# Moving the 1/rms multiply of gate and up to GpSimd in half of the feed-forward tiles

## The chip, the cores and the metric

The kernel runs on one core of a Trainium2 chip. The metric is the time of one execution on the device in microseconds (us). A core has engines that run side by side, each through its own instructions in order: TensorE (PE; its weight loads are shown as PEld), VectorE (DVE), ScalarE (ACT), GpSimd (POOL) and SyncE (SP), which here issues the loads. They wait for each other by semaphores. SBUF is the on-chip memory; PSUM is the small memory that TensorE writes its sums to.

## The reference

Two layers over 256 tokens of width 1024, in float32. Layer 0 mixes tokens with a short gated convolution, layer 1 with causal attention of 16 heads; each is followed by the same feed-forward, with 2816 gate and 2816 up channels:

```python
def conv_ffn(h, w_up, w_conv, w_down):
    gu = causal_dwconv(h @ w_up, w_conv)
    g, u = jnp.split(gu, 2, axis=-1)
    return (jax.nn.silu(g) * u) @ w_down

x = x + conv_ffn(rmsnorm(x, ffn_norm[i]), ffn_w_up[i], ffn_w_conv[i], ffn_w_down[i])
```

`rmsnorm` multiplies each token by 1/rms and each channel by a gain. The factor 1/rms belongs to the token, so it can be applied after the matmul with `w_up`, to gate and up, as long as it comes before the convolution over tokens.

## The kernel before

Activations lie with channels on the 128 partitions and the 256 tokens along the row. Each float32 matmul operand is split into a high and a low part, `hi` and `lo`, and three products are summed (high by high, high by low, low by high). Weights come from memory in units of 128 x 1024. `split_next` makes the two parts of the next unit: ScalarE copies it to `hi`, VectorE subtracts (`lo<-raw,hi`, the weight subtraction; both inputs in SBUF). Five units may be in flight (`SPLITS`), so VectorE can work ahead of TensorE by a few units and no more.

`ffn` (lines 660 to 727) runs both feed-forwards in 22 tiles `j` of 128 gate and 128 up channels. For a tile TensorE does the gate matmuls, the up matmuls, and from tile 4 on (`LAG_FFN`) the down projection of tile `j - 4`. Behind each of these pieces stands a `slot()`: it emits one `split_next`, and then the next step of every open task, oldest first. The steps of a tile are two generators:

- `gathered(j, h)`, once for gate and once for up: ScalarE copies one half of the PSUM sum into `gn`, VectorE adds the other half (`gn<-gu,gn`, one input in PSUM). After the add TensorE may use that PSUM bank again; there are banks for two tiles.
- `whole(j)`: first step, the multiply of `gn` by 1/rms (`gn<-gn,rstd`, 128 x 512, gate and up in one instruction). Second step, `taps`: ScalarE writes the first tap of gate and of up to `gy`, VectorE adds the two other taps (four `gy<-gn,sm,gy`, both tensor inputs in SBUF). Third: silu on ScalarE (`s`), times up on VectorE (`p`). Fourth: `p` is split for the down projection (`ps_jh` on ScalarE, `ps_jl` on VectorE).

So the multiply of tile `j` is emitted right behind the add of its up half; the next slot brings a weight subtraction and then the taps. The multiplies of tiles 0 and 1 are emitted together, since 1/rms (`rstd`) is ready only in tile 1. `V`, `S`, `G`, `E`, `Q` are VectorE, ScalarE, GpSimd, TensorE and SyncE, each wrapped in `InOrder`, which keeps the order of emission on that engine. GpSimd has one other job, eight multiplies by 1/rms in the mixer of layer 0 (`mix_cv`, line 591: `y<-y,rstd`, 128 x 256).

The multiply and what follows it (lines 676 to 679):

```python
            V.tensor_mul(gn, gn, nm.r[:, None, :].to_broadcast([P, 2, T]))
            yield
            taps(*((y[:, h, :], gn[:, h, :], partial(ffn_tap, layer, half=h, j=j)) for h in range(2)))
            yield
```

Of the kernel before, what the change touches and what calls it, by code (L numbers as in the profile page):

```python
# [15 lines left out]
P = 128  # L16
D = 1024
T = 256
# [4 lines left out]
NF = DFF // P  # L23
# [114 lines left out]
def trunk(ctx: ExitStack, tc: tile.TileContext, x, wall, small, ropes, masks, final, out):  # L138
    nc = tc.nc
    V, S, G, E, Q = (  # L140
        InOrder(tc, e) for e in (nc.vector, nc.scalar, nc.gpsimd, nc.tensor, nc.sync)
    )
# [103 lines left out]
    def unit(key):  # L246
        u = INDEX[key]
        while state["split"] <= u:
            split_next()
        return hi[u], lo[u]  # L250
# [4 lines left out]
    def spawn(*gens):  # L255
        tasks.extend(gens)

    def slot(splits=1, ahead=True):

        for _ in range(splits if ahead else 0):  # L260
            split_next()
        for g in sorted(tasks, key=lambda g: (g.__name__ == "rotate") == ahead):
            if next(g, StopIteration) is StopIteration:
                tasks.remove(g)
        for _ in range(0 if ahead else splits):
            split_next()

    def bank(name, tag="b"):
        return pp.tile([P, 2, T], F32, name=name, tag=tag, bufs=4)
# [68 lines left out]
    def table(func):  # L338

        t = line(ap_, 1, name="table", tag="table", bufs=1)  # L340
        S.activation(t, ones[:, 0:1], func)

    def finish_norm(i, nm, squared=False, tag="b"):

        ps = bank(f"ss{i}", tag=tag)
        for part, total in enumerate(nm.total):
            E.matmul(
                ps[:, 0, :], ones_r, total, start=part == 0, stop=part == 1, skip_group_check=True
            )
        rms = line(ap_, T, name=f"rms{i}", tag="rms", bufs=1)  # L350
        S.activation(rms, ps[:, 0, :], AF.Sqrt, bias=eps, scale=1.0 / D)
        nm.r = line(ap_, T, name=f"rstd{i}", tag="rstd", bufs=2)
        V.reciprocal(nm.r, rms)
        if squared:
            nm.r2 = ap_.tile([P, T], F32, name=f"rstd2{i}", tag="rstd2", bufs=1)
            V.tensor_mul(nm.r2, nm.r, nm.r)
# [29 lines left out]
    def project_both(dst, w, nm, ks=range(ND)):  # L386

        wh, wl = w
        kw = {"skip_group_check": True}
        for k in ks:  # L390
            s = slice(k * P, (k + 1) * P)
            E.matmul(
                dst.rearrange("p c t -> p (c t)"), wh[:, s], nm.both[k], start=k == 0, stop=False, **kw
            )
            E.matmul(dst[:, 0, :], wl[:, s], nm.xh[k], start=False, stop=k == ND - 1, **kw)
# [121 lines left out]
    def split_act(h, l, v):  # L517
        S.activation(h, v, AF.Copy)
        V.tensor_sub(l, v, h.bitcast(F32))

    def half_tile(name):
        return ap_.tile([P, T], F32, name=name, tag="t", bufs=NT)

    def pair_tile(name):
        return ap_.tile([P, 2, T], F32, name=name, tag="big", bufs=NBIG)

    def split_turned(name, v):

        h, l = (turned(name=name + c, tag="ps" + c, bufs=NPS) for c in "hl")
        split_act(h.places, l.places, by_place(v))  # L530
        return h.columns, l.columns

    def split_tiles(name, kind):
        return tuple(
            line(ap_, T, INPUTS_AT[kind], F32R, name=name + c, tag="ps" + c, bufs=NPS) for c in "hl"
        )

    def taps(*parts):

        for y, src, w in parts:  # L540
            S.activation(y, src, AF.Copy, scale=w(2))
        for t in (1, 0):
            o = 2 - t
            for y, src, w in parts:
                V.scalar_tensor_tensor(
                    y[:, o:], src[:, : T - o], w(t), y[:, o:], op0=ALU.mult, op1=ALU.add
                )
# [105 lines left out]
    nm = Norm()  # L653
# [6 lines left out]
    def ffn(layer, nm, i, then):  # L660
        acc, ps = (TokenAccum if then is None else Accum)(f"fo{layer}"), {}
        gus = {}
        tag = "ab"[then is not None]

        gns = {}

        def gathered(j, h):

            S.activation(gns[j][:, h, :], gus[j][h][:, 1, :], AF.Copy)
            V.tensor_add(gns[j][:, h, :], gus[j][h][:, 0, :], gns[j][:, h, :])  # L670
            yield

        def whole(j):
            gn, y = gns.pop(j), pair_tile(f"gy{layer}_{j}")
            s, p = half_tile(f"s{layer}_{j}"), half_tile(f"p{layer}_{j}")
            V.tensor_mul(gn, gn, nm.r[:, None, :].to_broadcast([P, 2, T]))
            yield
            taps(*((y[:, h, :], gn[:, h, :], partial(ffn_tap, layer, half=h, j=j)) for h in range(2)))
            yield
            S.activation(s, y[:, 0, :], AF.Silu)  # L680
            V.tensor_mul(p, s, y[:, 1, :])
            yield
            if layer == 0:
                ps[j] = split_turned(f"ps{layer}_{j}", p)
                return
            ps[j] = split_tiles(f"ps{layer}_{j}", f"down{layer}")
            split_act(*ps[j], p)

        for j in range(NF):
            if layer == 0 and j == 2:  # L690
                Q.dma_start(rope, ropes)
                Q.dma_start(mk, masks)
            gu = gus[j] = [bank(f"gu{layer}_{j}_{h}", tag=tag) for h in range(2)]
            gns[j] = pair_tile(f"gn{layer}_{j}")
            wg, wu = unit(("up", layer, 0, j)), unit(("up", layer, 1, j))
            if j == 0:
                for ks in ((0, 1), (2, 3), (4, 5), (6, 7)):
                    project_both(gu[0], wg, nm, ks)
                    project_both(gu[1], wu, nm, ks)
                spawn(gathered(0, 0), gathered(0, 1))  # L700
                if then is None:
                    spawn(turn(acc))
                slot()
                slot()
            else:
                project_both(gu[0], wg, nm)
                spawn(gathered(j, 0))
                slot()
                project_both(gu[1], wu, nm)
                spawn(gathered(j, 1))  # L710
                if j == 1:
                    finish_norm(i, nm, tag=tag)
                    table(AF.Silu)
                    spawn(whole(0))
                spawn(whole(j))
                slot()
            if j >= LAG_FFN:
                acc.add(("down", layer, j - LAG_FFN), ps[j - LAG_FFN], j == LAG_FFN, False)
                slot()
        last = range(NF - 2 - (then is None), NF)  # L720
        for j in range(NF - LAG_FFN, last[0]):
            acc.add(("down", layer, j), ps[j], False, False)
            slot()
        while tasks:
            slot(0)
        table(AF.Sqrt)
        acc.finish([("down", layer, j) for j in last], [ps[j] for j in last], then)
# [8 lines left out]
    nm = nm2  # L736
# [226 lines left out]
    def turn(acc):  # L963
        turn_pair(3)
        yield
        rows = blocks.rearrange("p (t q) m a -> p t q (m a)", t=2)
        moved = rest["moved"]
        for i in range(4):
            for q in range(4):
                Q.dma_start(  # L970
                    moved[32 * q : 32 * q + 32, :, i * T : (i + 1) * T], rows[32 * i : 32 * i + 32, :, q]
                )
            if i % 2:
                yield
        for _ in range(3):
            yield
        for t in range(2):
            for h in range(2):
                acc.seed(t, h, moved[:, t, h * 2 * T : (h + 1) * 2 * T])
            yield  # L980

    nm = Norm()
# [111 lines left out]
```

## Time and profile before

| | |
|---|---|
| median of 3 runs | 552.97 us (552.54 to 553.43) |
| profiled execution | 553.03 us |
| its span, first to last instruction | 551.1 us |
| TensorE busy in the span | 542.3 us (98%) |
| VectorE busy | 493.9 us (90%) |
| ScalarE busy | 370.9 us (67%) |
| GpSimd busy | 8.7 us (2%) |
| feed-forward of layer 0 / layer 1 | about 92 to 268 us / 372 to 545 us |

In a table of stretches the last three columns are the granted TensorE clock, the DMA share and GB/s. Rows of a timeline give the start in us from the span's start, the duration in us, the engine, the line, the operation, the tile that it writes and those that it reads, shapes, and a count where neighbours of one kind are merged; a bracket tells idle time of the engine in front of it and what ended it. Recorded neighbours on one engine overlap by about 0.08 us. All instructions carry line 121, that of the wrapper, so they are told apart by tiles. In the name `gn<-gn,rstd`, `rstd` is 1/rms.

### The profile page before, as it was taken

To read this page: it belongs to the slowest core of one execution; us is meant where nothing else is said; L and a number is where in the kernel's file an instruction comes from. 1 tells how busy PE (TensorE), PEld (TensorE's weight loads), DVE (VectorE), ACT (ScalarE), POOL (GpSimd) and SP (SyncE) were. 2 spreads that over 40 slices of the span, in tenths; PEclk is the share of its full clock that TensorE was granted. 3 is DMA by queue.
4 is the path that set the end of the run, shared out by engine and by line. 5 is a ranking of instruction groups with operands and counts; after the bars stand their busy time and mean duration, and the time that the engine had idled before them with its cause. 6 is when DMAs were issued, how large, how long until landed. Compare 5 with 4: busy or idle time off the path is not lost.

```text
span 551.1 us, 10100 instructions
## 1 busy us (share of the span) xinstructions
PE 542.3 (98%) x3911; PEld 509.0 (92%) x3911; DVE 493.9 (90%) x879; ACT 370.9 (67%) x652; POOL 8.7 (2%) x12
## 2 busy tenths in 40 slices
PE   8999999999999999999999999999999999999995
PEld 8999999889999999999999998999899999999985
DVE  6999777999999999999899887589999999889984
ACT  6746446767777766767856666677777777666655
POOL 0022000000000000000000000000000000000000
PEclk9999999999999999999999999999999999999998
DMA  8947653545665556556266244455665666655402
GB/s 294 399 165 292 228 173 144 205 161 213 227 217 216 219 200 223 195 188 227 84 225 230 78 153 153 154 211 218 208 219 212 218 221 222 223 195 188 152 0 79
DMA packets 18753, 107.85 MB, mean 196 GB/s; under 512 B 2192, under 2 KB 4880, under 8 KB 6544
## 3 DMA queue, kind: packets, MB, share of 16 engines
q1 hardware_dynamic: 18272, 106.65, 53.8%
q8 instruction: 31, 0.51, 0.3%
q10 hardware_dynamic: 432, 0.54, 0.3%
q14 instruction: 18, 0.15, 0.1%
HBM read 105.09 MB, written 1.05 MB: 193 GB/s over the span
## 4 chain that ended last, share of the span: by engine, by line
PE 87%; DVE 9%; ACT 1%; issue 1%; DMA 1%; SPq 0%; DVEq 0%; ACTq 0%
PE gu L121 33%; PE fo L121 20%; PE qk L121 8%; PE cv L121 7%; DVE lo L121 4%; PE ao L121 4%; PE v L121 4%; PE b L121 4%; PE mo L121 3%; DVE gy L121 2%; PE s L121 1%; DVE gn L121 1%; PE o L121 1%; PE pt L121 1%; DMA raw<-wall 1%
## 5 line engine op out<-in xcount | busy, mean ns | idle before, releaser
L121 DVE TENSOR_TENSOR lo<-raw,hi 128x1024 fp32r<-128x1024 f32 (+3 forms) x201 | 239.0, 1195 | 23.3 <-ACT hi L121 22.6
L121 ACT ACTIVATE hi<-raw 128x1024 fp32r<-128x1024 f32 (+2 forms) x199 | 205.2, 1040 | 51.6 <-PE gu L121 15.6
L121 PE MATMUL gu<-x,hi 128*128 128x512 f32 x704 | 233.0, 382 | 0.9 <-DVE gn L121 0.9
L121 PE MATMUL gu<-x,lo 128*128 128x256 f32 x704 | 192.1, 273 | 0.1
L121 PEld LDWEIGHTS gu<-x,hi 128*128 128x128 f32 x704 | 133.1, 189 | 19.3 <-DVE gn L121 1.5
L121 PEld LDWEIGHTS gu<-x,lo 128*128 128x128 f32 x704 | 135.1, 192 | 1.2 <-DVE lo L121 0.7
L121 DVE SCALAR_TENSOR_TENSOR gy<-gn,sm,gy 128x254 f32<-128x254 f32 (+1 forms) x176 | 72.9, 476 | 0.6 <-ACT gy L121 0.6
L121 ACT ACTIVATE gy<-gn,sm 128x256 f32<-128x256 f32 x88 | 39.8, 501 | 30.2 <-DVE gn L121 30.2
L121 PE MATMUL cv<-x,hi 128*128 128x256 f32 x256 | 44.5, 277 | 0.5 <-ACT hi L121 0.5
L121 PE MATMUL qk<-x,hi 128*128 128x256 f32 x256 | 43.8, 277 | 0.1
L121 ACT ACTIVATE gn<-gu 128x256 f32<-128x256 f32 x88 | 32.4, 371 | 14.9 <-PE gu L121 14.9
L121 PEld LDWEIGHTS cv<-x,hi 128*128 128x128 f32 x256 | 39.2, 193 | 0.8 <-ACT hi L121 0.7
L121 PEld LDWEIGHTS qk<-x,hi 128*128 128x128 f32 x256 | 38.8, 192 | 0.7 <-issue 0.6
L121 DVE TENSOR_TENSOR gn<-gu,gn 128x256 f32<-128x256 f32 x88 | 36.6, 418 | 0.6
L121 PE MATMUL qk<-x,lo 128*128 128x256 f32 x128 | 35.2, 275 | 0.0
L121 PE MATMUL cv<-x,lo 128*128 128x256 f32 x128 | 32.7, 277 | 0.4 <-DVE lo L121 0.4
L121 DVE TENSOR_TENSOR gn<-gn,rstd 128x512 f32<-128x512 f32 x44 | 30.2, 691 | 1.4
L121 ACT ACTIVATE s<-gy 128x256 f32<-128x256 f32 x44 | 18.2, 414 | 18.5 <-DVE gy L121 18.4
L121 PE MATMUL b<-x,hi 128*128 128x256 f32 x128 | 25.1, 275 | 0.0
L121 PEld LDWEIGHTS qk<-x,lo 128*128 128x128 f32 x128 | 24.6, 192 | 0.0
L121 PEld LDWEIGHTS cv<-x,lo 128*128 128x128 f32 x128 | 23.5, 193 | 0.6 <-DVE lo L121 0.6
L121 ACT ACTIVATE sm<-sm,nmx 128x256 f32<-128x256 f32 (+1 forms) x32 | 14.1, 442 | 12.5 <-DVE nmx L121 12.5
(484 smaller groups left out, 958.4 us busy)
## 6 DMA issues: line engine op xcount, KB each, us to landing
raw<-wall SPq DMA_DIRECT2D x95, 1024.0 KB, 4.8
raw<-wall SPq DMA_DIRECT2D x6, 384.0 KB, 6.5
late<-vts SPq DMA_DIRECT2D x16, 64.0 KB, 2.0
raw<-wall SPq DMA_DIRECT2D x3, 192.0 KB, 3.9
xt<-x SPq DMA_DIRECT2D x2, 256.0 KB, 6.2
late<-final SPq DMA_DIRECT2D x1, 512.0 KB, 5.6
out<-of SPq DMA_DIRECT2D x2, 256.0 KB, 2.2
rope<-ropes SPq DMA_DIRECT2D x1, 384.0 KB, 6.4
```

Of the source, the lines that this page charges most:

```text
L121: r = f(*args, **kw)
```

## The change

In tiles 0 to 10 of both feed-forwards (`NF` is 22) the multiply by 1/rms goes to GpSimd; in tiles 11 to 21 VectorE does it as before. Nothing else is touched: the same instruction on the same tiles, emitted at the same place.

```diff
-            V.tensor_mul(gn, gn, nm.r[:, None, :].to_broadcast([P, 2, T]))
+            (G if j < NF // 2 else V).tensor_mul(gn, gn, nm.r[:, None, :].to_broadcast([P, 2, T]))
```

## Rows read from the trace of the kernel before

**Rows 1.** The page, part 1: busy us (share of span), instructions, by engine.

```profile
PE 542.3 (98%) x3911; PEld 509.0 (92%) x3911; DVE 493.9 (90%) x879; ACT 370.9 (67%) x652; POOL 8.7 (2%) x12
```

**Rows 2.** Stretches: from:to, length, busy us (instructions) of PE, PEld, DVE, ACT, POOL.

```profile
97.00:110.00 13.00, 12.93 (x80) 11.66 (x79) 12.90 (x18) 9.40 (x16) 0.00 (x0) 1.00 0.60 214
110.00:133.00 23.00, 22.58 (x152) 20.77 (x151) 22.90 (x45) 16.14 (x32) 0.00 (x0) 1.00 0.49 180
...
150.00:175.00 25.00, 25.00 (x178) 23.65 (x177) 24.86 (x44) 18.00 (x32) 0.00 (x0) 1.00 0.65 239
...
380.00:394.00 14.00, 13.36 (x83) 12.06 (x82) 14.00 (x23) 9.50 (x18) 0.00 (x0) 1.00 0.49 149
...
480.00:532.00 52.00, 52.00 (x297) 47.14 (x296) 47.60 (x81) 35.04 (x60) 0.00 (x0) 1.00 0.42 154
```

**Rows 3.** Groups by line: instruction, count | busy us, mean ns | idle before.

```profile
L121 DVE TENSOR_TENSOR gn<-gn,rstd 128x512 f32<-128x512 f32 x44 | 30.2, 691 | 1.4
```

**Rows 4.** Timeline of POOL in the mixer; columns: start us, us, instruction.

```profile
33.04 0.73 POOL L121 TENSOR_TENSOR y<-y,rstd 128x256 f32<-128x256 f32 x1 [0.42 <-DVE y L121]
36.24 1.58 POOL L121 TENSOR_TENSOR y<-y,rstd 128x256 f32<-128x256 f32 x1 [2.47 <-DVE y L121]
```

**Rows 5.** Timeline of DVE beside those two multiplies.

```profile
33.26 0.42 DVE L121 TENSOR_TENSOR cv<-cv,cn 128x256 f32<-128x256 f32 x1
33.60 1.25 DVE L121 TENSOR_TENSOR lo<-raw,hi 128x1024 fp32r<-128x1024 f32 x1
...
36.01 1.22 DVE L121 TENSOR_TENSOR lo<-raw,hi 128x1024 fp32r<-128x1024 f32 x1
37.14 0.95 DVE L121 TENSOR_TENSOR ys0l<-yb,ys0h 128x256 fp32r<-128x256 f32 x1
```

**Rows 6.** Timeline of DVE around the multiply of tile 8, layer 0.

```profile
156.78 0.43 DVE L121 TENSOR_TENSOR gn<-gu,gn 128x256 f32<-128x256 f32 x1
157.25 0.69 DVE L121 TENSOR_TENSOR gn<-gn,rstd 128x512 f32<-128x512 f32 x1
157.85 1.22 DVE L121 TENSOR_TENSOR lo<-raw,hi 128x1024 fp32r<-128x1024 f32 x1
158.99 1.66 DVE L121 SCALAR_TENSOR_TENSOR gy<-gn,sm,gy 128x255 f32<-128x255 f32 x4
160.57 1.22 DVE L121 TENSOR_TENSOR lo<-raw,hi 128x1024 fp32r<-128x1024 f32 x1
```

**Rows 7.** Timeline of ACT behind that multiply: the first taps.

```profile
157.97 0.91 ACT L121 ACTIVATE gy<-gn,sm 128x256 f32<-128x256 f32 x2 [1.18 <-DVE gn L121]
```

**Rows 8.** Timeline of DVE around the multiply of tile 3, layer 0.

```profile
122.06 0.41 DVE L121 TENSOR_TENSOR gn<-gu,gn 128x256 f32<-128x256 f32 x1
...
126.22 0.45 DVE L121 TENSOR_TENSOR gn<-gu,gn 128x256 f32<-128x256 f32 x1
```

**Rows 9.** Timeline of DVE around the multiplies of tiles 0 and 1, layer 0.

```profile
106.69 1.16 DVE L121 TENSOR_TENSOR lo<-raw,hi 128x1024 fp32r<-128x1024 f32 x1
...
108.10 1.28 DVE L121 TENSOR_TENSOR gn<-gn,rstd 128x512 f32<-128x512 f32 x2
...
113.59 0.41 DVE L121 TENSOR_TENSOR gn<-gu,gn 128x256 f32<-128x256 f32 x1
```

**Rows 10.** Timeline of PE: the first matmul with each of three lo units.

```profile
133.48 0.38 PE L121 MATMUL gu<-x,lo 128*128 128x256 f32 x1
...
181.10 0.27 PE L121 MATMUL gu<-x,lo 128*128 128x256 f32 x1
...
462.28 0.38 PE L121 MATMUL fo<-lo,ps_8h 128*128 128x512 f32 x1
```

**Rows 11.** Timeline of DVE: the subtractions that wrote those three units.

```profile
132.20 1.22 DVE L121 TENSOR_TENSOR lo<-raw,hi 128x1024 fp32r<-128x1024 f32 x1
...
174.74 1.22 DVE L121 TENSOR_TENSOR lo<-raw,hi 128x1024 fp32r<-128x1024 f32 x1
...
454.06 1.22 DVE L121 TENSOR_TENSOR lo<-raw,hi 128x1024 fp32r<-128x1024 f32 x1
```

## The prediction

> **What bounds the kernel now.** The page comes first: TensorE is busy for 98% of the span and VectorE for 90% [rows 1]. With both so full, a share says nothing; what matters is who waits for whom, stage by stage. The table by stretches shows that TensorE loses time in two places of the feed-forwards only, at the start of each [rows 2]: 12.93 of 13.00 us busy from 97 to 110, 22.58 of 23.00 from 110 to 133, 13.36 of 14.00 from 380 to 394. VectorE has no gap there (14.00 of 14.00). From 150 to 175 TensorE is full and VectorE still has no gap; from 480 to 532 VectorE has 4.4 us to spare. So VectorE enters each feed-forward late, is just fast enough, works its way ahead of TensorE, and idles once its buffers are full. The first eleven tiles, where the change acts, are the ones in which it has no gap.
>
> How fast it gains is read from one tile in its order of time [rows 6]. The weight subtraction behind tile 8's taps starts at 160.57 us, the one behind tile 10's at 174.74 [rows 11]: 7.1 us a tile. TensorE first uses the one behind tile 4's taps at 133.48 and that behind tile 10's at 181.10 [rows 10]: 7.9 us a tile. VectorE gains 0.8 us a tile. Behind tile 4 its slack is nothing (132.20 + 1.22 = 133.42, used at 133.48); behind tile 10 it is 181.10 - 175.96 = 5.14 us. In layer 1 the subtraction behind tile 10's taps ends at 455.28 and is first used at 462.28: 7.00 us. (Which subtraction feeds which matmul is found by counting, since both engines take the weight units in the plan's order.)
>
> **What is removed.** 11 multiplies in each layer, 0.69 us each [rows 3]. They take 0.64 us from the add's end to the start of the next instruction (157.21 to 157.85) [rows 6], 22 x 0.64 = 14.1 us of VectorE.
>
> **What is added, and what GpSimd's rows say of it.** GpSimd does the same kind of multiply in the mixer, at half this size [rows 4]. Undisturbed it takes 0.73 us (at 33.04). Issued while VectorE runs a weight subtraction it takes 1.58 (at 36.24, one of three such), and ends 0.59 after that subtraction (37.82 against 37.23) [rows 4, 5]. So it waits for that instruction, and then needs 0.59. The reverse shows as well. Behind the subtraction at 36.01, the next VectorE instruction, ys0l, is issued at 37.14 and takes 0.95, where cv, of the same size, takes 0.42; it ends 0.28 after GpSimd is done. The subtraction at 33.60 ends 1.08 after the GpSimd multiply that ran when it was issued. But a VectorE instruction with one operand in PSUM, cv at 33.26, is not lengthened beside that multiply. Two SBUF operands on VectorE and a GpSimd multiply exclude each other for a whole instruction, and a GpSimd multiply that waits gets in between two VectorE instructions.
>
> The Trainium skill has two wordings of this. "Advanced Engine Details and Errata", section VectorE Performance Modes, names GpSimd interference for VectorE's two-port modes alone; by it these float32 two-input instructions would run undisturbed, and the change would give the faster rival below. "SBUF — State Buffer", section Who interferes with whom, adds VectorE instructions with two SBUF inputs against a GpSimd instruction that reads SBUF. The 0.95 us of ys0l decides for the second.
>
> **The multiply's length at 512 elements** is in no row. Call C the time it holds VectorE off once a running subtraction ends. Upper bound: 1.46, twice the undisturbed 0.73. Proportional to the 0.59: 1.18. Lower bound: 0.59 plus what 256 more elements cost VectorE, 0.69 - 0.41 = 0.28, so 0.87. I take 1.15, just under proportional: the 0.14 by which 0.73 exceeds 0.59 is a fixed part already taken out, and it equals VectorE's own fixed part (2 x 0.41 - 0.69 = 0.13). By "GPSIMD Engine Reference" of the Trainium skill, section Elementwise — side-by-side cycle accounting (2048 elements in 4497 ns, an estimate of 2.2 ns each), C would also be 1.15 and the sum the same; no run here shows it.
>
> **One tile worked through (tiles 5 to 10).** Let T be the end of the add that completes gn (157.21 in rows 6). Now: multiply, subtraction, four taps, next subtraction at 160.57 = T + 3.36. After the change VectorE, which issues in order, goes straight to the subtraction, at T - 0.08 (neighbours overlap by 0.08). GpSimd starts some 0.23 behind it (36.24 against 36.01 in the mixer), finds the subtraction running, and gets in at T + 1.14. It ends at T + 1.14 + C. ScalarE's first tap starts 0.03 later, as it does now behind the multiply [rows 7], and takes 0.50; VectorE's taps start 0.03 after that and need 1.58 to the next subtraction (158.99 to 160.57). That lands at T + 3.28 + C. VectorE loses C - 0.08 = 1.07 us a tile, 6.4 in six tiles. What waits behind the taps on VectorE is the next weight subtraction, and TensorE waits for that one. ScalarE's next weight copy, queued behind its two taps, ends near T + 3.0 + C, before VectorE asks for it; that costs nothing as long as it stays under T + 3.28 + C.
>
> **Tiles 3 and 4** have a ps subtraction of some 0.4 us between weight subtraction and taps, which fills part of the wait. Now the next instruction comes at 126.22, with T = 122.47: T + 3.75 [rows 8]. After: T + 3.28 + C again. Loss C - 0.47 = 0.68 each, 1.4 for the two. Tile 2 has two ps subtractions; with another 0.38 hidden it loses 0.3.
>
> **Tiles 0 and 1** are multiplied back to back at 108.10 [rows 9], and the add that lets TensorE go on comes at 113.59. After: GpSimd takes tile 0 when the subtraction ends at 107.85, until 109.00. The next subtraction, held off, ends 1.08 later, at 110.08. GpSimd takes tile 1 until 111.23. The first tap ends 0.28 after it, seven more follow at 0.395, and the add starts at 114.20: 0.6 late. Dropping two multiplies (1.3) has not paid for two exclusions (2.3), less what a PSUM add and the overlaps hide.
>
> **The sum.** VectorE is behind its present schedule by 0.6 + 0.3 + 1.4 + 6.4 = 8.7 us after tile 10. Layer 0: 8.7 less the slack of 5.14 is 3.55 us of TensorE waiting, most of it early, where the slack is nothing. Layer 1, by the same tile costs: 8.7 - 7.00 = 1.7. From tile 11 on VectorE has its multiply back and catches up 0.8 a tile for eleven tiles, which just covers it; I cost the end of the layer at nothing, and if the cover fails it is tenths of a us. Together 5.2. The profiled execution took 553.03 (span 551.1 and 1.9 around it), level with the median of 552.97: **558.2 us**.
>
> **Bounds.** Each 0.1 us of C is 2.2 us of the result while both layers are late. C = 0.87 gives 8.7 - 3.1 = 5.6 us behind: 0.5 to 0.8 us in layer 0, nothing in layer 1, 553.7. C = 1.46 gives 12.1 behind: 7.0 + 5.1, so 565.
>
> **Rivals.**
> 1. Faster: no exclusion at this operand shape, GpSimd runs beside VectorE. Its multiply would end near T + 0.15 + 1.3 = T + 1.45, the taps start near T + 2.0 against T + 1.78 now (157.21 to 158.99): 0.2 lost a tile in tiles 5 to 10, which the slack hides, and 1.3 us won at tiles 0 and 1, where TensorE waits. The gain is at most what TensorE loses there, 0.07 + 0.42 + 0.64 = 1.1 us [rows 2]: 551.9. It decides if a VectorE instruction with two SBUF operands keeps its length beside a GpSimd multiply. For it: VectorE is the late engine in just these tiles. Against: ys0l's 0.95. Chance 0.09.
> 2. No change: C is near its lower bound, so slack swallows nearly all: 553.5. For it: nothing but the lack of a 512-element row. Chance 0.08.
> 3. Forecast, slower: 0.83. In it, about 0.08 lies above 563: C near 1.4, or VectorE's ps subtraction getting in ahead of GpSimd, or the end of a layer not caught up.
>
> The range that holds 8 in 10 leaves out the faster rival and the top: 554.5 to 563. A measurement of this kernel can tell about 0.2%, 1.1 us, from no change; the chances for faster, the same and slower by that are 0.09, 0.08 and 0.83.
>
> **What would show it.** On the page: 22 GpSimd multiplies gn<-gn,rstd of about 2.1 us each (0.15 after T to T + 2.29), where 1.3 would mean no exclusion. VectorE idle in front of the first tap, ended by ScalarE's tap, some 1.7 us a tile in tiles 5 to 10. Weight subtractions and taps themselves little longer than now, since the loss is waiting. TensorE waiting for lo in tiles 4 to 11 of layer 0 and less in layer 1. From tile 11 on, tiles of the present length. Wrong would be: subtractions beside GpSimd at 1.22 us with GpSimd at 1.3 (rival 1), or a layer 1 that loses as much as layer 0 (its slack misread).

## The result, and the profile after

The changed kernel takes 560.82 us (560.61 to 561.30) against 552.78 us in the same comparison: ratio 1.0145, 95% interval 1.0133 to 1.0157, 8.0 us slower. The forecast was 558.2, 5.2 us slower, in a range of 554.5 to 563. The profiled execution took 560.87 us, its span is 558.6.

Three lines of the page after: busy time by engine (as [rows 1]), then two groups, with busy us, mean ns of one, and the idle time in front of them.

```profile
PE 545.6 (98%) x3911; PEld 508.9 (91%) x3911; DVE 483.6 (87%) x857; ACT 368.1 (66%) x652; POOL 57.2 (10%) x34
...
L121 DVE SCALAR_TENSOR_TENSOR gy<-gn,sm,gy 128x254 f32<-128x254 f32 (+1 forms) x176 | 75.1, 489 | 28.2 <-ACT gy L121 28.2
...
L121 POOL TENSOR_TENSOR gn<-gn,rstd 128x512 f32<-128x512 f32 x22 | 48.5, 2208 | 334.9 <-DVE rstd L121 233.1
```

VectorE fell from 90 to 87% busy, and TensorE stayed at 98%: the shares would let one expect a gain. The second line has the cost. In front of the taps VectorE now sits idle for 28.2 us, ended by ScalarE's first tap. GpSimd's multiply of 128 x 512 is recorded with 2.2 us. The taps in the kernel before, with 0.6 us of idle time:

```profile
L121 DVE SCALAR_TENSOR_TENSOR gy<-gn,sm,gy 128x254 f32<-128x254 f32 (+1 forms) x176 | 72.9, 476 | 0.6 <-ACT gy L121 0.6
```

The table by stretches (columns as in [rows 2]; layer 1 begins 4.5 us later than before):

```profile
97.00:110.00 13.00, 12.90 (x80) 11.65 (x79) 12.90 (x17) 9.05 (x15) 3.21 (x2) 1.00 0.62 216
110.00:133.00 23.00, 20.87 (x139) 18.74 (x138) 20.18 (x37) 13.28 (x26) 8.48 (x4) 1.00 0.45 158
133.00:150.00 17.00, 15.99 (x111) 14.61 (x111) 12.84 (x22) 10.94 (x20) 4.63 (x3) 1.00 0.53 198
150.00:175.00 25.00, 25.00 (x174) 23.06 (x173) 19.75 (x35) 16.30 (x30) 6.44 (x3) 1.00 0.56 189
390.00:404.00 14.00, 12.82 (x79) 11.58 (x78) 12.83 (x20) 8.09 (x18) 7.03 (x3) 1.00 0.58 189
480.00:532.00 52.00, 52.00 (x297) 47.23 (x296) 51.76 (x90) 38.08 (x68) 0.00 (x0) 1.00 0.57 209
```

TensorE was busy 20.87 of 23.00 us from 110 to 133 (before 22.58), 15.99 of 17.00 from 133 to 150 (before 16.93), and 12.82 of 14.00 from 390 to 404 (before, from 386 to 400, 13.36). VectorE had no gap in these tiles before; from 150 to 175 it now works 19.75 of 25.00 us, and yet it is what TensorE waits for. At the end of layer 1 (480 to 532) it has no idle time left (51.76 of 52.00, before 47.60): it is catching up.

One tile of the changed kernel, tile 7 of layer 0, beside [rows 6] (a tile of the same kind): GpSimd's timeline, with tile 3's multiply above it, and then VectorE's.

```profile
123.74 2.52 POOL L121 TENSOR_TENSOR gn<-gn,rstd 128x512 f32<-128x512 f32 x1 [4.46 <-DVE gn L121]
...
155.54 2.12 POOL L121 TENSOR_TENSOR gn<-gn,rstd 128x512 f32<-128x512 f32 x1 [6.01 <-DVE gn L121]
```

```profile
154.98 0.41 DVE L121 TENSOR_TENSOR gn<-gu,gn 128x256 f32<-128x256 f32 x1
155.31 1.21 DVE L121 TENSOR_TENSOR lo<-raw,hi 128x1024 fp32r<-128x1024 f32 x1
158.24 1.67 DVE L121 SCALAR_TENSOR_TENSOR gy<-gn,sm,gy 128x255 f32<-128x255 f32 x4 [1.72 <-ACT gy L121]
159.82 1.22 DVE L121 TENSOR_TENSOR lo<-raw,hi 128x1024 fp32r<-128x1024 f32 x1
```

The add ends at 155.39 = T. VectorE starts the weight subtraction at once, GpSimd at 155.54; the subtraction ends at 156.52, GpSimd's multiply at 157.66, 1.14 us after it. The taps start at 158.24, after 1.72 us without work, and the next subtraction at 159.82 = T + 4.43. Before, it came at T + 3.36.

Where TensorE waits: first its wait for the add behind tiles 0 and 1 of layer 0 in the kernel before, then all its waits over 0.5 us in the feed-forwards of the changed kernel, and one of the short ones late in layer 1 (timeline of TensorE; the bracket is idle time and what ended it; the last row has none because the modelled end of the matmul before it hides the gap of 0.19):

```profile
114.06 0.48 PE L121 MATMUL gu<-x,hi 128*128 128x512 f32 x1 [0.27 <-DVE gn L121]
```

```profile
114.57 0.48 PE L121 MATMUL gu<-x,hi 128*128 128x512 f32 x1 [0.85 <-DVE gn L121]
...
130.03 0.38 PE L121 MATMUL fo<-ps_1h,lo 128*128 128x256 f32 x1 [1.07 <-DVE lo L121]
...
136.69 0.38 PE L121 MATMUL gu<-x,lo 128*128 128x256 f32 x1 [1.01 <-DVE lo L121]
...
398.94 0.48 PE L121 MATMUL gu<-x,hi 128*128 128x512 f32 x1 [1.18 <-DVE gn L121]
...
406.67 0.48 PE L121 MATMUL fo<-hi,ps_0h 128*128 128x512 f32 x1 [0.93 <-ACT fo L121]
...
469.67 0.48 PE L121 MATMUL fo<-lo,ps_8h 128*128 128x512 f32 x1
```

The length of a feed-forward's gate and up work, from the start of its first such matmul to that of its last, shows by layer where time went. The stretch from there to the next stage was 13.5 and 13.3 us (within 0.1), and the middle between the feed-forwards 103.7, in every kernel here but one. The first two rows differ by 4.6 and 2.95 us, which leaves 0.3 of the 7.8 between the two profiled executions. Outside the spans they differ by 0.4 (2.26 against 1.89 us; other kernels here had 1.78 to 2.11), and no run explains that. The medians are from three comparisons, in which the kernel before took 552.78 to 552.90 us; each difference below is taken within one of them. How far VectorE is behind is read from the same weight subtraction in two kernels, each time counted from the start of the layer's gate and up work.

| kernel (GpSimd multiplies in tiles ...) | median us | layer 0, us | layer 1, us |
|---|---|---|---|
| before (none) | 552.9 | 162.59 | 160.34 |
| after (0 to 10) | 560.82 | 167.18 | 163.29 |
| t0_1 (0, 1) | 554.03 | 163.12 | 160.89 |
| t2_4 (2 to 4) | 557.33 | 165.30 | 161.54 |
| t5_10 (5 to 10) | 554.26 | 163.87 | 160.35 |
| t11_16 (11 to 16) | 552.88 | 162.58 | 160.35 |
| t11_20 (11 to 20) | 562.91 | 162.57, then 6.0 late | 160.35, then 4.5 late |
| dead_mul | 559.48 | 166.73 | 162.64 |
| dead_set | 552.78 | 162.63 | 160.32 |
| later_g (2 to 10) | 553.60 | 163.00 | 160.35 |
| later_v (none) | 552.04 | 161.84 | 160.35 |
| later_v1 (none) | 551.38 | 161.77 | 159.52 |

### The profile page after: what moved, and what is told of

Same layout as the page of the kernel before. It is cut to its first block, busy times and chain, and to the rows that moved or that the text cites. A ratio compares the mean times of both kernels' runs of the same rounds, so it can differ in the third digit from the quotient of the medians.

```text
span 558.6 us, 10112 instructions
## 1 busy us (share of the span) xinstructions
PE 545.6 (98%) x3911; PEld 508.9 (91%) x3911; DVE 483.6 (87%) x857; ACT 368.1 (66%) x652; POOL 57.2 (10%) x34
## 3 DMA queue, kind: packets, MB, share of 16 engines
HBM read 105.09 MB, written 1.05 MB: 190 GB/s over the span
## 4 chain that ended last, share of the span: by engine, by line
PE 85%; DVE 7%; ACT 3%; POOL 2%; issue 1%; DMA 1%; SPq 0%; DVEq 0%; ACTq 0%; POOLq 0%
PE gu L121 32%; PE fo L121 20%; PE qk L121 8%; PE cv L121 7%; PE ao L121 4%; PE v L121 4%; PE b L121 4%; PE mo L121 3%; DVE lo L121 3%; POOL gn L121 2%; DVE gy L121 2%; ACT hi L121 1%; PE s L121 1%; PE o L121 1%; DMA raw<-wall 1%
## 5 line engine op out<-in xcount | busy, mean ns | idle before, releaser
L121 DVE SCALAR_TENSOR_TENSOR gy<-gn,sm,gy 128x254 f32<-128x254 f32 (+1 forms) x176 | 75.1, 489 | 28.2 <-ACT gy L121 28.2
L121 POOL TENSOR_TENSOR gn<-gn,rstd 128x512 f32<-128x512 f32 x22 | 48.5, 2208 | 334.9 <-DVE rstd L121 233.1
L121 ACT ACTIVATE s<-gy 128x256 f32<-128x256 f32 x44 | 18.3, 416 | 13.3 <-DVE gy L121 12.5
```

The source lines that it names most:

```text
L121: r = f(*args, **kw)
```

## The experiments

**Is it the exclusion, or the wait for GpSimd's result?** Two kernels leave VectorE's multiplies where they were and add a GpSimd instruction behind the taps, where nothing reads `gn` any more. In the first it repeats the multiply, in the second it writes zeros.

```diff
             taps(*((y[:, h, :], gn[:, h, :], partial(ffn_tap, layer, half=h, j=j)) for h in range(2)))
+            if j < NF // 2:
+                G.tensor_mul(gn, gn, nm.r[:, None, :].to_broadcast([P, 2, T]))
             yield
```

> VectorE keeps all multiplies. In tiles 0 to 10 GpSimd repeats the multiply on gn behind the taps, where nobody reads gn any more, so that nothing waits for GpSimd's result and the output is the same. A (exclusion): each holds back one VectorE instruction with two SBUF operands by some 1.1 us (less what a PSUM add hides, 0.3), without giving 0.64 back, so VectorE loses 0.8 to 1.1 a tile: 9 to 12 us late, less 5.15 and 7.0 of slack: +4 to +12, centre +7, 560. Theory C (what costs is the wait for GpSimd's result through ScalarE, not the exclusion): nothing waits, 0, 552.8.

Measured: 559.48 us, ratio 1.0121 (1.0106 to 1.0135), 6.6 slower, near the centre of theory A. Nothing waits for this multiply, and yet it costs nearly as much as the change: exclusion costs time by itself. GpSimd and VectorE in tile 5 of layer 0:

```profile
137.46 2.47 POOL L121 TENSOR_TENSOR gn<-gn,rstd 128x512 f32<-128x512 f32 x1 [5.71 <-ACT s L121]
```

```profile
137.23 1.22 DVE L121 TENSOR_TENSOR lo<-raw,hi 128x1024 fp32r<-128x1024 f32 x1
138.37 0.42 DVE L121 TENSOR_TENSOR p<-s,gy 128x256 f32<-128x256 f32 x1
138.70 0.42 DVE L121 TENSOR_TENSOR gn<-gu,gn 128x256 f32<-128x256 f32 x1
139.03 1.98 DVE L121 TENSOR_TENSOR lo<-raw,hi 128x1024 fp32r<-128x1024 f32 x1
```

The subtraction at 137.23 and p behind it keep their lengths, and GpSimd waits. It gets in at about 138.79, where p (both inputs in SBUF) ends and the add, with one input in PSUM, runs its usual 0.42. The next subtraction takes 1.98 in place of 1.22: it ends at 141.01, 1.08 after GpSimd's end at 139.93, the same 1.08 as in the mixer [rows 4, 5].

The two costs are not alike, though, for dead_mul leaves VectorE its multiply. In tiles 5 to 10 of layer 0 VectorE fell 0.76 us behind a tile there. In the changed kernel it fell 1.05 behind a tile although 0.64 us of work had gone, and it stood idle in front of the taps. What the exclusion makes of that idle time is an estimate: GpSimd takes 1.28 us for this multiply when nothing holds it up (last section), so in tile 7 it would have ended at 156.82 and not at 157.66. That is 0.84 of the 1.72 us; without it some 0.2 of the 1.05 would be left, as rival 1 had it. The rest of the wait is GpSimd's own time and ScalarE's tap.

```diff
+            if j < NF // 2:
+                G.memset(gn, 0.0)
```

> As the one before, but GpSimd writes a constant to gn (128 x 512) in place of the multiply: the same place, the same wait, the same bytes written, none read. The output is the same. If exclusion is over reading two operands in SBUF: GpSimd runs beside VectorE, weight subtractions stay at 1.22 us, 0 (within 0.3), 552.8. If it is over any GpSimd access to SBUF: some 0.5 us held off a tile, VectorE 5 us late, +1 to +3.

Measured: 552.78, ratio 0.9997 (0.9988 to 1.0006): no cost.

```profile
139.44 0.53 POOL L121 MEMSET gn<- 128x512 f32 x1 [6.53 <-ACT s L121]
```

```profile
139.23 1.22 DVE L121 TENSOR_TENSOR lo<-raw,hi 128x1024 fp32r<-128x1024 f32 x1
140.37 0.42 DVE L121 TENSOR_TENSOR p<-s,gy 128x256 f32<-128x256 f32 x1
```

GpSimd writes 128 x 512 elements in 0.53 us while the subtraction at 139.23 runs, and that one keeps its 1.22. So GpSimd does not exclude VectorE merely by running; the two GpSimd instructions differ in that one reads SBUF (and in operation and length, which these runs do not part from it). The Trainium skill draws the line at reading ("SBUF — State Buffer", section Who interferes with whom): a VectorE instruction with two SBUF inputs contends with a GpSimd instruction that reads SBUF, not with one that only writes it. This pair of traces agrees, with 1.98 against 1.22 us.

**What each group of tiles costs.** Four kernels differ from the one before in the condition alone:

```diff
-            V.tensor_mul(gn, gn, nm.r[:, None, :].to_broadcast([P, 2, T]))
+            (G if j < 2 else V).tensor_mul(gn, gn, nm.r[:, None, :].to_broadcast([P, 2, T]))
```

> GpSimd multiplies in tiles 0 and 1 of each feed-forward alone. Theory A (exclusion on VectorE, less the slack that VectorE has against TensorE): in the changed kernel the add that releases TensorE behind these tiles came 0.5 us late, and the slack there is 0.06 in both layers, so 0.5 + 0.5 = +1.0 us, 553.8. Theory B (each of the 22 moved multiplies costs TensorE the same, 8.0 / 22 = 0.36 us, wherever it stands): 4 x 0.36 = +1.5, 554.2. Either way the trace tells them apart by the stall in layer 0 at 113 us (0.5 longer under A). Rival 1 of the prediction (no exclusion): -1.

Measured: 554.03, ratio 1.0024 (1.0015 to 1.0032), 1.1 slower: 0.53 in layer 0 and 0.55 in layer 1, near theory A's 1.0. The wait behind these tiles, 0.27 us in the kernel before, is 0.85, as in the changed kernel. The time alone does not exclude B, whose 1.5 lies inside the interval (0.8 to 1.8 us); the next two kernels do.

The next two have `G if 2 <= j < 5` and `G if 5 <= j < 11`.

> GpSimd multiplies in tiles 2 to 4 alone. A: in the changed kernel these three tiles cost VectorE 0.7 + 1.0 + 1.0 = 2.7 us in layer 0, where the slack is 0.06, so +2.6; in layer 1 the cost is 2.8 and the slack 2.3, so +0.5; together +3.1, 555.9. With the prediction's own sizes for these tiles (0.3 + 0.7 + 0.7, the ps subtractions behind GpSimd) it would be 1.6 in layer 0 and nothing in layer 1, 554.4. B: 6 x 0.36 = +2.2, 555.0.

Measured: 557.33, ratio 1.0082 (1.0068 to 1.0096), 4.4 slower, more than either theory gave. Layer 0 grew by 2.7, as A has it. Layer 1 grew by 1.2, not 0.5. ScalarE and TensorE in that place:

```profile
401.75 0.91 ACT L121 ACTIVATE gy<-gn,sm 128x256 f32<-128x256 f32 x2 [2.46 <-POOL gn L121]
402.56 0.36 ACT L121 ACTIVATE gn<-gu 128x256 f32<-128x256 f32 x1
402.83 1.05 ACT L121 ACTIVATE hi<-raw 128x1024 fp32r<-128x1024 f32 x1
403.78 1.11 ACT L121 ACTIVATE fo<-late 128x512 f32<-128x512 f32 x2
```

```profile
404.42 0.48 PE L121 MATMUL fo<-hi,ps_0h 128*128 128x512 f32 x1 [0.92 <-ACT fo L121]
```

In layer 1 ScalarE copies the residual into the down projection's accumulators (`fo<-late`), in order behind tile 2's taps. The taps waited for GpSimd until 401.75, so the copies came at 403.78, 2.0 us behind the taps' start as before, and TensorE waited 0.92 us for them. That is a queue I had not looked at. In the profiled execution another 0.65 us stands behind the last matmul: SyncE waits 2.7 us there for the last output transfer (us in all, times, longest), where it waits 2.1 in the kernel before. Why that transfer took longer stays open.

```profile
SPq L1089 <- DMA out<-of: 2.7, 1, 2.7
```

> GpSimd multiplies in tiles 5 to 10 alone, the tiles in which one multiply costs VectorE most (1.05 us). A: 6.3 us late against a slack that has grown to 5.15 in layer 0: +1.1; in layer 1 6.4 against 7.0: 0. Together +1.1, 553.9. B: 12 x 0.36 = +4.4, 557.2.

Measured: 554.26, ratio 1.0024 (1.0014 to 1.0034), 1.4 slower: 1.28 in layer 0, 0.01 in layer 1. Twelve multiplies, each costing VectorE 1.05 us, cost TensorE a tenth of their sum; A's 1.1 lies in the interval (0.8 to 1.9), B's 4.4 does not.

`G if 11 <= j < 21`:

> GpSimd multiplies in tiles 11 to 20 alone, nearly as many as in the changed kernel, where VectorE is ahead by 6 to 8 us. A: each costs VectorE 1.05 us as before, 0.8 of it is what VectorE gains a tile or idles, so some 0.25 a tile of slack is used up and TensorE never waits: 0 (-0.3 to +0.4), 552.8. B: 20 x 0.36 = +7.3, 560.1.

Measured: 562.91, ratio 1.0161 (1.0141 to 1.0182), 10 slower: the reverse of what A had predicted, and nearer to B's 560.1, which the interval excludes too. The five runs spread from 559.97 to 563.83 us, with a granted clock from 0.998 down to 0.988, and the profiled one is the longest of them. The table above shows that neither is right. Gate and up work took exactly as long as before in both layers; the loss is behind it. TensorE's waits from 250 us on, and TensorE around the first of the two (stretch, us, busy (instructions), granted clock, DMA share, GB/s):

```profile
PE fo L121 <- ACT ps_21h L121: 4.9, 2, 2.8
```

```profile
263.00:266.00 3.00, 0.84 (x6) 0.92 0.85 325
266.00:269.00 3.00, 2.58 (x12) 0.50 0.55 180
...
273.00:278.00 5.00, 5.00 (x47) 1.00 0.00 0
```

TensorE waits for ps of tile 21, the last tile. I had counted VectorE's lead in weight units and PSUM banks and left out that the last tile's own chain (add, multiply, taps, p, ps) has nothing in front of it: in the kernel before it ends 0.4 us before TensorE asks for it. VectorE must have caught up by then. Against the kernel before, it lost some 1.07 us a tile in tiles 11 to 13 of layer 0 and 0.23 to 0.35 a tile from there on, where the rest of each loss fell into time that it would have idled. It was 5.05 us behind after tile 20, and the one tile left gave back 0.84. In layer 1 it was 4.4 behind. The two waits come to 4.9 us; most of the rest is TensorE's clock, below.

`G if 11 <= j < 17` puts the amended theory to the test, with as many tiles as t5_10:

> GpSimd multiplies in tiles 11 to 16 alone: as many as in tiles 5 to 10, which cost 1.4 us, and six of the ten that cost 10 us in tiles 11 to 20, where TensorE waited for the last tile at the end of each layer and nowhere before. A, amended: VectorE falls 6.3 us behind; in the kernel before it has some 7 us without work from tile 12 to the end of layer 0 and about as much in layer 1, so it has caught up by the last tile: 0 in layer 0, 0 to 0.5 in layer 1, 552.9 to 553.4. If the loss at the end came from the late tiles' own chain and not from the time behind, tiles 11 to 16 cost 0 as well, but VectorE shows its idle time between tile 17 and the end unchanged; A has it shrink by some 6 us. If every GpSimd multiply in these tiles costs the same (10 / 20 = 0.5 us): +6, 559.

Measured: 552.88, ratio 0.9999 (0.9990 to 1.0008): the multiplies that cost 1.4 us in tiles 5 to 10 are free here. VectorE from tile 17 on (stretch, us, busy (instructions), granted clock, DMA share, GB/s), here and then in the kernel before:

```profile
225.00:250.00 25.00, 24.86 (x43) 1.00 0.63 219
250.00:268.00 18.00, 15.28 (x28) 1.00 0.62 224
```

```profile
225.00:250.00 25.00, 23.10 (x38) 1.00 0.56 191
250.00:268.00 18.00, 14.67 (x26) 1.00 0.55 205
```

It was idle for 1.9 and 3.3 us in these stretches before, 5.2 together, and 2.9 now. That the idle time shrinks speaks for A, but by 2.4, not by 6: VectorE was only 4.15 us behind after tile 16 (its subtraction for tile 18 has a slack of 3.67 us where the kernel before has 7.82), because its lead before had been capped by full buffers: tiles 14 to 16 cost it 0.25 to 0.34 each, tiles 11 to 13 1.06 to 1.13. By tile 21 it was level with the kernel before.

**Can the wait be filled?** Two kernels emit the taps of tiles 2 to 10 one slot later, with GpSimd's multiply in those tiles and, as the control, with VectorE's.

```diff
-            V.tensor_mul(gn, gn, nm.r[:, None, :].to_broadcast([P, 2, T]))
+            (G if 2 <= j < 11 else V).tensor_mul(gn, gn, nm.r[:, None, :].to_broadcast([P, 2, T]))
             yield
+            if 2 <= j < 11:
+                yield
```

> GpSimd multiplies in tiles 2 to 10, and the taps of these tiles are emitted one slot later, so that VectorE has a weight subtraction or more to do where it waited for GpSimd and ScalarE. Tiles 0 and 1 are as before. A: the wait goes and the exclusion stays: 1.14 held off less 0.64 given back, 0.5 a tile in place of 1.05. VectorE gains 0.8 a tile from tile 5 on, so only tiles 2 to 4 count: 1.5 less nothing in layer 0, and nothing in layer 1: +1.5, 554.3. C (only the wait costs): VectorE is 0.64 a tile better off, -0.5 to -1.5, 552.

> The control for the one before: taps of tiles 2 to 10 one slot later, all multiplies on VectorE. VectorE does the same work in another order: 0 (within 0.4), 552.8 by every theory.

Measured: later_g 553.60, ratio 1.0013 (1.0004 to 1.0022); later_v 552.04, ratio 0.9984 (0.9975 to 0.9993). Against its control GpSimd's multiply costs 1.6 us. The number is A's, the reason is not. VectorE's waits (us in all, times, longest), GpSimd and VectorE in one tile of layer 0:

```profile
DVE gy L121 <- ACT gy L121: 21.1, 13, 1.7
```

```profile
159.19 3.66 POOL L121 TENSOR_TENSOR gn<-gn,rstd 128x512 f32<-128x512 f32 x1 [4.88 <-DVE gn L121]
```

```profile
159.03 1.21 DVE L121 TENSOR_TENSOR lo<-raw,hi 128x1024 fp32r<-128x1024 f32 x1
160.16 0.42 DVE L121 TENSOR_TENSOR ps_7l<-p,ps_7h 128x256 fp32r<-128x256 f32 x1
160.50 1.21 DVE L121 TENSOR_TENSOR lo<-raw,hi 128x1024 fp32r<-128x1024 f32 x1
163.43 0.48 DVE L121 SCALAR_TENSOR_TENSOR gy<-gn,sm,gy 128x255 f32<-128x255 f32 x1 [1.71 <-ACT gy L121]
```

In 13 of the 18 tiles VectorE still stood idle in front of the taps, for up to 1.7 us. The later slot put two more instructions with two SBUF inputs behind the first subtraction, and GpSimd, ready at 159.19, waited for all three; it got in when VectorE stopped at 161.71, and VectorE stopped because it needed GpSimd's result. The wait had moved by a slot. Tiles 2 and 3 of layer 1, where no such wait stood, cost next to nothing; by the end of tile 10 VectorE was 6.4 us behind its control in layer 0 and 7.5 in layer 1, where the same tiles of the changed kernel had lost it 9.0 and 9.2. The slack takes all of this in layer 1 and all but 1.2 us in layer 0. It is larger early on, since the later taps let weight subtractions run earlier, which the control shows by itself: the subtraction that ends at 133.42 us in the kernel before, 0.06 ahead of its use, has 1.4 us of slack there.

**A version that beats both.** The control moves 0.75 us out of layer 0's start. The add that frees TensorE in tile 4 still stands behind eight taps, so tile 1's taps go one slot later too (`if 1 <= j < 11`, all multiplies on VectorE).

> All multiplies on VectorE; the taps of tiles 1 to 10 one slot later (in later_v: of tiles 2 to 10). The add that releases TensorE in tile 4 (114.0 us in the kernel before) then stands behind four taps and no longer behind eight, 1.6 us earlier, where TensorE waited 0.4 in layer 0 and 0.8 in layer 1. If the order of emission on VectorE sets these stalls, both go: 552.0 - 1.2 = 550.8, below both kernels. If another wait takes their place (ps of tile 1, a weight subtraction): 552.0.

Measured: 551.38, ratio 0.9971 (0.9960 to 0.9982), 1.5 us below the kernel before and 9.4 below the changed one. Stretches, columns as in [rows 2]:

```profile
110.00:133.00 23.00, 22.84 (x155) 21.20 (x154) 22.90 (x45) 16.27 (x31) 0.00 (x0) 1.00 0.53 184
380.00:394.00 14.00, 14.00 (x89) 12.90 (x88) 14.00 (x23) 9.64 (x18) 0.00 (x0) 1.00 0.50 152
```

The 0.64 us of [rows 2] from 380 to 394 are gone (14.00 of 14.00), and 0.26 of the 0.42 from 110 to 133. Both stalls went, but the time is 551.4 and not 550.8: against later_v layer 1 won 0.83 us and layer 0 only 0.07, since another wait, for a weight subtraction, took the place of the stall there:

```profile
130.10 0.38 PE L121 MATMUL gu<-x,lo 128*128 128x256 f32 x1 [0.16 <-DVE lo L121]
```

The same work in another order won time where the move to another engine lost it.

## Why the prediction was right, and where its sizes were off

1. **The exclusion** was read rightly from eight multiplies in the mixer; dead_mul and dead_set show it apart from the wait for GpSimd's result. Rival 1 is out.
2. **C**, taken as 1.15 from rows of half the size, measured 1.14 (157.66 less 156.52). The fixed part is the same as in the mixer: 1.28 us alone (last section) less 1.14 is 0.14, as 0.73 less 0.59 was. GpSimd's recorded length in tiles 5 to 10 is 2.12 to 2.19 against the 2.1 forecast. "GPSIMD Engine Reference" of the Trainium skill, section Elementwise — side-by-side cycle accounting, gives 4497 ns for 2048 elements. By that, an estimate of 2.2 ns an element, and the 0.59 us of the mixer, C would be 1.15; the trace agrees.
3. **Tiles 5 to 10**: T + 4.43 was forecast for the next subtraction (3.28 + 1.15) and is what the trace has. Loss 1.07 a tile forecast, 1.05 measured over six tiles. The idle time in front of the taps, forecast at 1.7, is 1.72.
4. **Tiles 0 and 1**: 0.6 forecast, 0.5 measured (0.54 of TensorE's time in layer 1, 0.53 and 0.55 in t0_1).
5. **Tiles 2 to 4** are the mis-sized term. The prediction said that a GpSimd multiply that waits gets in between two VectorE instructions, and let it run ahead of the ps subtraction. In tile 3:

```profile
123.25 0.41 DVE L121 TENSOR_TENSOR gn<-gu,gn 128x256 f32<-128x256 f32 x1
123.58 1.21 DVE L121 TENSOR_TENSOR lo<-raw,hi 128x1024 fp32r<-128x1024 f32 x1
124.72 0.43 DVE L121 TENSOR_TENSOR ps_2l<-p,ps_2h 128x256 fp32r<-128x256 f32 x1
126.84 1.67 DVE L121 SCALAR_TENSOR_TENSOR gy<-gn,sm,gy 128x255 f32<-128x255 f32 x4 [1.70 <-ACT gy L121]
128.43 0.42 DVE L121 TENSOR_TENSOR gn<-gu,gn 128x256 f32<-128x256 f32 x1
```

ps_2l follows the subtraction without a gap, takes its usual 0.43 and ends at 125.15; GpSimd (123.74 + 2.52) ends at 126.26, 1.11 later. The ps subtraction fills no wait, it makes it 0.4 longer. The add comes at 128.43 = T + 4.77 (T = 123.66), not T + 4.43. These tiles lost 0.66, 1.0 and 1.0 us in place of 0.3, 0.68 and 0.68. The prediction held this case possible and left it out of the centre, on the strength of ys0l alone. In sum VectorE was 9.5 us behind after tile 10 of layer 0, not 8.7, and the first matmul with that subtraction came 4.4 us later: 0.8 of the 1.0 by which layer 0 was short (4.6 against 3.55). Of the other 0.2, 0.1 is the earlier start of the layer (92.00 against 92.09 us), and 0.1 came at the next matmul but is not explained.
6. **Layer 1** was costed with layer 0's tiles. It lost 9.8 us by tile 10, of which 7.0 were slack: 2.8 of the 2.95 measured, against 1.7. Tile 2 lost 1.1 there: both of its ps subtractions went ahead of GpSimd. The 0.93 us at 406.67, ScalarE's late accumulator copies, are not added to this: with them TensorE was 1.7 us late, and the subtractions' own lateness, less their slack, passed that at tile 7 (6.57 - 4.64 = 1.93). So they would have brought the same delay by 469. t2_4 shows the copies by themselves.
7. **ScalarE's queue at nothing**: right for the weight copy, and wrong for these copies.
8. **The end of the layer at nothing**: right (13.51 and 13.29 us, unchanged), but by little. VectorE did not gain on the kernel before until tile 14, where that one began to idle, and then 0.8 us a tile; in layer 1 it drew level with TensorE only behind tile 20. t11_20 shows what a failed cover costs there: not tenths, but 4.5 to 6 us.

## What to carry to other kernels

Moving an instruction to an idle engine can cost more than it saves when the two engines shut each other out: here 0.69 us of VectorE became 1.14 us in which VectorE could read no second SBUF operand, GpSimd had to wait for a VectorE instruction first, and the result came back through another engine's queue. Cost such a move per tile along the in-order queues, and then subtract the lead that the late engine has at that tile; the lead is spent once, it is nothing at a stage's start, and at the stage's end it has to be back. When an engine is late at the start of a stage, first ask whether its queue can be put in another order.

## What the runs showed of the hardware that was not expected

- **Who goes first.** When GpSimd and VectorE both wait for SBUF reads, neither always wins. Behind a running subtraction, p and ps went ahead of a waiting GpSimd multiply (p in dead_mul's tiles, ps_2l above), up to three instructions in a row in later_g; ys0l [rows 5], the first VectorE tap of tile 0 in the changed kernel and the second ps subtraction of tile 2 in layer 0, among others, were held back behind it. In the changed kernel, dead_mul and later_g a waiting GpSimd multiply got in every time VectorE ran an instruction with a PSUM input or stopped. What decides in the other cases stays open.
- **GpSimd alone**: once in the changed kernel (408.49 us) it found VectorE waiting and took 1.28 us for 128 x 512, against 0.73 for half of that [rows 4]: 0.55 us for 256 more elements. In dead_mul, six that started beside an add with a PSUM input took 1.27 to 1.30.
- **A wait can cost twice.** In t11_20 the granted clock fell to 0.50, the lower level of 1.2 GHz, after TensorE had stood idle for 2.2 us in front of ps of tile 21, and was back at 1.00 by 273 us. Its matmuls of 256 columns started 0.21 us apart there, and 0.11 apart before the wait. In the changed kernel, whose waits were at most 1.2 us each, it stayed at 1.00 in all stretches shown.
